# Experts of a decoder layer: five split weight halves of six, a written order for three engines, twelve raw pages

## The chip, the cores and the metric

The kernel runs on one core of one Trainium2 chip. The metric is device microseconds of one execution, median of three runs: 1540.11 us before the change (1538.99 to 1541.56).

## What is computed

One decoder layer over 1024 tokens of width 1024: an RMSNorm and a combined input projection, stick-breaking attention and an S5 state-space branch side by side, a gated merge and output projection, then a hierarchical mixture of experts and a final RMSNorm. The change is in the mixture of experts only:

```python
def hierarchical_moe(x, rg_w, rg_b, re_w, re_b, w1, w3, w2):
    # router: top-1 of 4 groups, then top-2 of the 8 experts in it; gate = p_group * softmax
    ...
    # each of the 32 experts: (silu(xe @ w1) * (xe @ w3)) @ w2, w1 and w3 1024 x 512, w2 512 x 1024
    ...
```

Tokens are routed in blocks of 128 rows: every expert takes the first 128 tokens that chose it; a rare overflow is handled in a branch at the end. All weights are float32.

## The kernel before

From 0 to about 862 us the kernel does everything ahead of the experts; the last part of that is a loop over eight token tiles that adds the output projection, writes the normed tokens to `hg_d` and computes the routing. Then `moe` runs 32 experts, one after the other, and ends with a sum over each token's two results, the final norm and the stores.

**An expert's weights** are six pages of 1 MB, halves of w1, w3 (k-blocks 0 to 3 and 4 to 7) and w2, loaded by SP's queue (L1052) into a ring of 14 raw pages: six named r, six m, two x. A load waits until its page is given back. A half is then either *split* or used *natively*. Split (`split`, L98 to L102): ScalarE copies it to a high part in fp32r (L101, CAST), VectorE subtracts that to make a low part (L102, TENSOR_TENSOR), and TensorE makes three fp32r products per k-block, high by high, high by low, low by high. Native: TensorE multiplies the float32 page itself (L1120, two records for each product). Before, the first halves of w1 and w3 and both halves of w2 are split, four of six; the second halves of w1 and w3 are native. Split parts live in three pairs of pages: two of name w, one of name ms.

**An expert's steps.** GpSimd gathers its 128 tokens by an indirect DMA (L1066). TensorE transposes them (L1088); ScalarE and VectorE make xh and xl (four k-blocks) and xf, the unsplit rest. `up` (L1112 to L1114 split, L1120 native) forms the two products a1 and a3; ScalarE's sigmoid (L1126) and two VectorE products (L1128) form the hidden tile in `mid`; TensorE transposes that (L1133), ScalarE and VectorE split it to hh and hl, and `down` (L1145 to L1147) multiplies by w2 into the two banks o0 and o1. ScalarE scales by the gate (L1152), GpSimd scatters the rows to `ye_d` (L1159). The last two experts' results stay on the chip.

**What sets the order.** `moe` is written with `down` one expert behind `up`; within that a scheduler, which simulates the engines, chose each engine's order when the kernel was built. Engines are in order, so what stands in front of a late instruction's followers holds them. For the first expert the lows of both first units are made on GpSimd (`HELD`, L102 with POOL), as routing occupies VectorE; and the first pages are loaded during the routing.

Of the kernel before, what the change touches and what calls it, by code (L numbers as in the profile page):

```python
# [22 lines left out]
D = 1024  # L23
# [10 lines left out]
NE = 32  # L34
# [960 lines left out]
def moe(tc, ctx, pool, i, ident, rt, ye_d, tab_d, h2_d, hg_d, split, con, out, rp, mp, wop, wop1, scale):  # L995
# [4 lines left out]
    XG, YB, NX, LAG = 3, 4, 2, 3  # L1000
    PS = (1, 3, 5)
    XL = 3, 3, 5, 5, 7, 7
    INIT = RING = 12 + NX
    HELD = 2
    LAST = 2
    with ExitStack() as c:
# [6 lines left out]
        xg, ss = row[:XG], p.tile([128, FF], F32, name="mid", bufs=1)  # L1013
# [9 lines left out]
        def add(key, ap, shape):  # L1023
            num[key] = len(src)
            src.append((ap, shape))

        for e in range(NE + 1):
            for u in range(2):
                for j, w in enumerate(w13):
                    if e < NE:  # L1030
                        add((e, u, j), w[e, :, u * 4:u * 4 + 4, :], [128, 4, FF])
            for u in range(2):
                if e:
                    add((e - 1, u, 2), w2[e - 1, :, u * 2:u * 2 + 2, :], [128, 2, D])
# [10 lines left out]
        def ring(n, shape, r=False):  # L1045
            k = n if n < INIT else (n - INIT) % RING
            return page(*((rp, "r", 6) if k < 6 else (mp, "m", MR) if k < 12 else (p, "x", NX)), shape, r)
# [28 lines left out]
        with tc.issue_after(rt["hold"]):  # L1076
            for n in range(HELD):
                unit(n)

        def xt(e):  # L1080

            x = xg[e % XG]
            xh, xl = (p.tile([128, 4, 128], F32R, name=n, bufs=1) for n in ("xh", "xl"))
            xf = p.tile([128, 4, 128], F32, name="xf", bufs=1)
            for q in range(2):
                tp = ps.tile([128, 4, 128], F32, name="tr", bufs=2)
                for k in range(4):
                    nc.tensor.transpose(tp[:, k], x[:, (q * 4 + k) * 128:(q * 4 + k) * 128 + 128], ident)  # L1088
                if q:
                    A.copy(xf, tp)  # L1090
                else:
                    parts[:] = split(xh, xl, tp)
            return xh, xl, xf

        gather(0)
        parts = []
        X = {0: xt(0)}
        read = rt["finish"](first[0], parts[1])
        with tc.issue_after(read):
            for n in range(12, INIT):  # L1100
                load(n)
        for n in range(1, XG):
            gather(n)
        for n in range(INIT, INIT + HELD):
            load(n)

        def up(e, xh, xl, xf):
            a = [ps.tile([128, 512], F32, name=n, bufs=2) for n in ("a1", "a3")]
            for w in range(2):
                h, l = unit(num[e, 0, w])  # L1110
                for k in range(4):
                    nc.tensor.matmul(a[w], lhsT=xh[:, k], rhs=h[:, k], start=(k == 0), stop=False)  # L1112
                    nc.tensor.matmul(a[w], lhsT=xh[:, k], rhs=l[:, k], start=False, stop=False)  # L1113
                    nc.tensor.matmul(a[w], lhsT=xl[:, k], rhs=h[:, k], start=False, stop=False)  # L1114
            yield
            for w in range(2):
                n = num[e, 1, w]
                load(n)
                for k in range(4):
                    nc.tensor.matmul(a[w], lhsT=xf[:, k], rhs=raws[n][:, k], start=False, stop=(k == 3))  # L1120
            yield

            s = ss.rearrange("p (k q) -> p k q", k=4)
            a = [x.rearrange("p (q k) -> p k q", k=4) for x in a]
            r = _f(tab[:, e, 3:4])
            A.activation(s, a[0], AF.Sigmoid, scale=r)  # L1126
            for n in range(2):
                V.scalar_tensor_tensor(s, a[n], r, s, op0=OP.mult, op1=OP.mult)  # L1128

        def ht():  # L1130
            tp = ps.tile([128, 4, 128], F32, name="tr", bufs=2)
            for k in range(4):
                nc.tensor.transpose(tp[:, k], ss[:, k * 128:k * 128 + 128], ident)  # L1133
            rooted[:] = split(hh, hl, tp)

        def down(e):
            o = [ps.tile([128, 512], F32, name=f"o{n}", bufs=1) for n in range(2)]
            for u in range(2):
                with tc.issue_after(rooted[0]) if e == NE - 1 and u else ExitStack():
                    h, l = unit(num[e, u, 2])  # L1140
                for n in range(2):
                    cs = slice(n * 512, n * 512 + 512)
                    for k in range(2):
                        kk = u * 2 + k
# [51 lines left out]
        for e in range(NE):  # L1196
            g = up(e, *X[e])
            next(g)
            if e:
                ht()  # L1200
# [201 lines left out]
```

## Time and profile before

| | us |
|---|---|
| median of 3 runs | 1540.11 |
| profiled execution, its own time | 1539.6 |
| its span in the profile | 1537.7 |
| TensorE busy | 1456.8 |
| VectorE busy | 963.0 |
| ScalarE busy | 722.3 |
| GpSimd busy | 518.9 |

The experts take from about 865 to 1493 us of the span, the part after them some 45 us. The mean granted TensorE clock is 0.974 of full speed. The DMA engines read 284.03 MB and write 44.11 MB; most of the reading is the experts' weights, in the last 16 of the profile's 40 slices. The span and the profiled execution's own time differ by 1.9 us; the profiled execution is 0.5 us under the median.

### The profile page before, as it was taken

The page shows a single profiled execution, that of the slowest core. Times are in us where ns is not written, and L with a number is a line of the kernel's source. Part 1 is how long each engine was busy: PE and PEld are TensorE (multiplying, and loading weights), DVE is VectorE, ACT ScalarE, POOL GpSimd, SP SyncE. Part 2 cuts the span into 40 slices and gives each one's busy share as a digit, 9 for nine tenths or more (in the row PEclk, how much of TensorE's full clock was granted, in tenths as well). Part 3 has the DMA queues.
Part 4 walks back from the last instruction along what each step waited for, and adds up shares of the span by engine and source line. Part 5 has one row for each costly group of instructions (what it writes and reads, how often), then busy time and mean ns, then how long its engine had stood idle before and what let it go on. Part 6 is the DMA issues. An engine that isn't in the chain of part 4 may idle for free. (4 is left out here: it accounts for less than half of the span.)

```text
span 1537.7 us, 19509 instructions
## 1 busy us (share of the span) xinstructions
PE 1456.8 (95%) x6900; PEld 1123.4 (73%) x6900; DVE 963.0 (63%) x1488; ACT 722.3 (47%) x1141; POOL 518.9 (34%) x542
## 2 busy tenths in 40 slices
PE   7989799999999989999998799999999999999986
PEld 6967688998888867778787566666666666666663
DVE  6757565465756568665578566666665566656547
ACT  6212122455656577432223255555555455555543
POOL 1199941144444465332255321111111111111034
PEclk8999899999999999999999799999999999999998
DMA  8242344211111015264763799999999989999754
GB/s 256 77 104 72 92 104 97 60 42 54 30 51 34 28 44 142 78 198 160 268 247 124 286 346 356 352 354 353 356 360 351 353 342 358 334 334 357 271 200 163
DMA packets 132197, 314.77 MB, mean 205 GB/s; under 512 B 24305, under 2 KB 82289, under 8 KB 107522
## 3 DMA queue, kind: packets, MB, share of 16 engines
q1 hardware_dynamic: 120898, 295.99, 55.0%
q0 software_dynamic: 9728, 16.83, 2.9%
q8 instruction: 55, 0.90, 0.2%
q10 hardware_dynamic: 1472, 0.69, 0.2%
q14 instruction: 44, 0.36, 0.1%
HBM read 284.03 MB, written 44.11 MB: 213 GB/s over the span
## 5 line engine op out<-in xcount | busy, mean ns | idle before, releaser
L134 PE MATMUL mm<-xh,wh 128*128 128x512 f32 (+4 forms) x608 | 224.1, 369 | 1.1 <-DVE kl L691 0.6
L135 PE MATMUL mm<-xl,wh 128*128 128x512 f32 (+4 forms) x608 | 222.6, 366 | 0.0
L136 PE MATMUL mm<-xh,wl 128*128 128x512 f32 (+4 forms) x608 | 221.3, 364 | 0.8 <-DVE wl L102 0.8
L1159 POOL DMA_INDIRECT ye_d<-w,tab x32 | 56.1, 1754 | 250.0 <-ACT w L1152 249.4
L134 PEld LDWEIGHTS mm<-xh,wh 128*128 128x128 f32 x608 | 115.4, 190 | 16.0 <-issue 1.1
L136 PEld LDWEIGHTS mm<-xh,wl 128*128 128x128 f32 x608 | 115.4, 190 | 14.9 <-DVE wl L102 1.5
L135 PEld LDWEIGHTS mm<-xl,wh 128*128 128x128 f32 x608 | 115.3, 190 | 13.9 <-DVE xl L225 0.4
L754 DVE TENSOR_TENSOR_SCAN pr<-pr 128x144 f32<-128x144 f32 (+3 forms) x64 | 92.6, 1448 | 46.8 <-POOL pr L751 46.1
L102 DVE TENSOR_TENSOR w<-m,w 128x2048 fp32r<-128x2048 f32 x38 | 88.9, 2342 | 40.8 <-ACT w L101 40.7
L102 DVE TENSOR_TENSOR w<-r,w 128x2048 fp32r<-128x2048 f32 x36 | 82.2, 2291 | 47.6 <-ACT w L101 47.2
L1066 POOL DMA_INDIRECT w<-hg_d,tab x31 | 34.8, 1122 | 222.0 <-PE tr L1088 217.1
L755 POOL TENSOR_TENSOR be<-be,pr 128x143 f32<-128x143 f32 (+3 forms) x64 | 89.4, 1400 | 38.4 <-DVE pr L754 36.0
L1120 PE MATMUL a<-r,xf 128*128 128x512 f32 x224 | 100.7, 592 | 0.0
L1120 PE MATMUL a<-m,xf 128*128 128x512 f32 x208 | 93.3, 592 | 0.0
L1128 DVE SCALAR_TENSOR_TENSOR mid<-a,tab,mid 128x512 f32<-128x512 f32 x64 | 47.9, 749 | 63.8 <-ACT mid L1126 52.0
L101 ACT CAST w<-r 128x2048 fp32r<-128x2048 f32 x38 | 72.1, 1903 | 27.5 <-PE a L1113 14.4
L101 ACT CAST w<-m 128x2048 fp32r<-128x2048 f32 x38 | 72.5, 1907 | 18.9 <-PE o L1146 10.3
L101 ACT CAST wh<-wr 128x1024 fp32r<-128x1024 f32 (+1 forms) x44 | 44.6, 1014 | 65.8 <-PE mm L135 57.3
L1120 PEld LDWEIGHTS a<-r,xf 128*128 128x128 f32 x224 | 41.8, 190 | 42.3 <-issue 40.4
L102 DVE TENSOR_TENSOR wl<-wr,wh 128x1024 fp32r<-128x1024 f32 (+1 forms) x44 | 57.1, 1297 | 23.6 <-ACT wh L101 23.5
L1146 PE MATMUL o<-w,w 128*128 128x512 f32 x172 | 68.6, 399 | 3.2 <-DVE w L102 3.2
L751 POOL TENSOR_SCALAR_AFFINE_SELECT pr<-pr 128x128 f32<-128x128 f32 x64 | 26.3, 411 | 132.9 <-ACT pr L748 113.1
(534 smaller groups left out, 3766.2 us busy)
## 6 DMA issues: line engine op xcount, KB each, us to landing
r<-in_w_dram SPq DMA_DIRECT2D x84, 1024.0 KB, 7.9
m<-in_w_dram SPq DMA_DIRECT2D x82, 1024.0 KB, 8.1
x<-in_w_dram SPq DMA_DIRECT2D x26, 1024.0 KB, 7.9
wr<-in_w_in_dram SPq DMA_DIRECT2D x32, 512.0 KB, 4.2
gate_d<-gt SPq DMA_DIRECT2D x32, 256.0 KB, 2.3
x<-in_x_dram SPq DMA_DIRECT2D x8, 512.0 KB, 4.6
y<-y_d SPq DMA_DIRECT2D x16, 256.0 KB, 3.2
wr<-in_w_out_dram SPq DMA_DIRECT2D x8, 512.0 KB, 4.3
```

Source lines behind the costliest of these rows:

```text
L101: a = (A if heng is None else heng).copy(h, src)
L102: return a.ins, (V if leng is None else leng).tensor_sub(l, src, _f(h)).ins
L134: nc.tensor.matmul(ps, lhsT=wh, rhs=xh, start=first, stop=False)
L135: nc.tensor.matmul(ps, lhsT=wh, rhs=xl, start=False, stop=False)
L136: nc.tensor.matmul(ps, lhsT=wl, rhs=xh, start=False, stop=last)
L754: V.tensor_tensor_scan(rv, rv, rv, 1.0, op0=OP.mult, op1=OP.bypass)
L755: P.tensor_mul(be[:, :W - 1], be[:, :W - 1], pr[:, 1:W])
L1066: q = P.indirect_dma_start(out=xg[e % XG], out_offset=None, in_=hg_d, in_offset=IO(ap=tab[:, e, 0:1] if e else rt["idx"], axis=0), bounds_ ...
L1120: nc.tensor.matmul(a[w], lhsT=xf[:, k], rhs=raws[n][:, k], start=False, stop=(k == 3))
L1128: V.scalar_tensor_tensor(s, a[n], r, s, op0=OP.mult, op1=OP.mult)
L1146: nc.tensor.matmul(o[n], lhsT=hh[:, kk], rhs=l[:, k, cs], start=False, stop=False)
L1159: put = P.indirect_dma_start(out=ye_d, out_offset=IO(ap=tab[:, e, 1:2], axis=0), in_=y, in_offset=None, bounds_check=2 * S - 1, oob_is_err ...
```

## The change

Within `moe`, and nowhere else:

- Weights: the second half of w1 is split too. Five of six halves are split; only w3's second half is native, 4 native products per expert where there were 8, and 60 split products where there were 48. xh and xl now hold all eight k-blocks.
- Pages: the two raw x pages become a fourth pair for split parts, and the pairs go round in the order x, w, w, ms. The raw ring has 12 pages, r and m.
- Order: a `manual_schedule` for TensorE, ScalarE and VectorE; their instructions are issued as the loop writes them. In iteration e: gate scaling and scatter of e−2; up(e,w1,0); up(e,w3,0); half of the transposes of e+1; the hidden tile of e−1 transposed and split; up(e,w1,1); the other transposes; down(e−1,0); the native half; down(e−1,1). Loads are issued in the order of use.
- The hidden tile is written in the row of the expert's result; the tile `mid` is gone.
- Start: units (0,w1,0) and (0,w3,0) have their lows on GpSimd, the first in pair x, the second in pair w; unit (0,w1,1) has its low on VectorE.
- End: as the engines' orders stand, both w2 halves of expert 31 are split ahead of the overflow branch, and the result of expert 30 is split behind it. Two of the eight tiles of `ye_d` rows go to x pages.

```diff
@@ constants
-    XG, YB, NX, LAG = 3, 4, 2, 3
+    XG, YB, LAG = 3, 4, 3
-    INIT = RING = 12 + NX
+    RING = 12
@@ units
-        def unit(n):
-            if n not in units:
-                load(n)
-                pl, nm, b = (mp, "ms", 2) if len(units) % 3 == 2 else (wop, "w", 4)
-                h, l = units[n] = [view(pl.tile([128, 4, FF], F32R, name=nm, bufs=b), src[n][1]) for _ in range(2)]
-                split(h, l, raws[n], leng=P if n < HELD else V)
-            return units[n]
+        PAIRS = (p, "x", 2), (wop, "w", 4), (wop, "w", 4), (mp, "ms", 2)
+        def unit(*key, other=False, later=False):
+            n = num[key]
+            load(n)
+            h, l = units[key] = [page(*PAIRS[len(units) % 4], src[n][1], True) for _ in range(2)]
+            A.copy(h, raws[n])
+            low = lambda: (P if other else V).tensor_sub(l, raws[n], _f(h))
+            return low if later else low()
@@ the order
+        with tc.manual_schedule(engines={mybir.EngineType.PE, mybir.EngineType.Activation, mybir.EngineType.DVE}):
+            unit(0, 0, 1)
+            for e in range(NE):
+                more = e + 1 < NE
+                acc[e] = [ps.tile([128, 512], F32, name=n, bufs=2) for n in ("a1", "a3")]
+                if e >= 2:
+                    result(e - 2)
+                up(e, 0, 0)
+                if e:
+                    unit(e - 1, 2, 0)
+                up(e, 1, 0)
+                if e:
+                    low = unit(e - 1, 2, 1, later=True)
+                if more:
+                    tp = xt(e + 1, 0)
+                if e:
+                    th = turn(ys(e - 1), 0)
+                if more:
+                    xparts(tp, 0)
+                if e:
+                    split(hh, hl, th)
+                    low()
+                if more:
+                    unit(e + 1, 0, 0)
+                up(e, 0, 1)
+                if more:
+                    tp = xt(e + 1, 1)
+                    xparts(tp, 1)
+                    unit(e + 1, 1, 0)
...
+                if e:
+                    down(e - 1, 0)
+                if more:
+                    unit(e + 1, 0, 1)
+                native(e)
+                mid = middle(e)
+                next(mid)
+                if more:
+                    A.copy(xf, tp)
+                drain(mid)
+                if e:
+                    down(e - 1, 1)
...
         overflow(at)
-        ht()
-        parted()
+        th = turn(ys(NE - 1), 0)
+        rooted[:] = split(hh, hl, th)
+        result(NE - 2)
+        for u in range(2):
+            unit(NE - 1, 2, u)
```

How the instructions stand. In the names, a is a product of `up`, o one of `down`, tr a bank of transposes, w_86.. a row tile (tokens, result or hidden parts), r, m, x, w, ms the pages.

TensorE in the middle of a steady expert, around one native half; before:

```order
L1114 MATMUL a_9242<-w,xl 128x512
L1133 MATMUL tr<-ident,mid 128x128 x3
L1112 MATMUL a_9243<-w,xh 128x512
L1133 MATMUL tr<-ident,mid 128x128
L1120 MATMUL a_9242<-r,xf 128x512 x4
L1088 MATMUL tr<-ident,w_8634 128x128
L1113 MATMUL a_9243<-w,xh 128x512
```

and after:

```order
L1095 MATMUL tr<-ident,w_8635 128x128 x4
L1136 MATMUL o_9537<-ms,w_8641 128x512
...
L1138 MATMUL o_9538<-ms,w_8641 128x512
L1116 MATMUL a_9447<-r,xf 128x512 x4
L1136 MATMUL o_9537<-x,w_8641 128x512
L1137 MATMUL o_9537<-x,w_8641 128x512
```

Before, native products and transposes stand between split products of the same bank; after, the one native half stands whole between the two halves of `down` (L1136 to L1138), in every expert alike.

ScalarE over one expert; before:

```order
L101 CAST ms<-m 128x2048
L101 CAST xh<-tr 128x512
L1090 COPY xf<-tr 128x512
L101 CAST w<-m 128x2048
L1152 ACTIVATE w_8637<-o_9077,tab 128x512
L101 CAST w<-x 128x2048
L1152 ACTIVATE w_8637<-o_9078,tab 128x512
L101 CAST ms<-x 128x2048
L101 CAST w_8641<-tr 128x512
L1126 ACTIVATE mid<-a_9120,tab 128x512
```

and after:

```order
L1145 ACTIVATE w_8639<-o_9404,tab 128x512
L1145 ACTIVATE w_8639<-o_9405,tab 128x512
L1067 CAST ms<-r 128x2048
L1067 CAST x<-r 128x2048
L101 CAST xh<-tr 128x512
L101 CAST w_8641<-tr 128x512
L1067 CAST w<-r 128x2048
L101 CAST xh<-tr 128x512
L1067 CAST w<-r 128x2048
L1067 CAST ms<-m 128x2048
L1123 ACTIVATE w_8637<-a_9446,tab 128x512
L1236 COPY xf<-tr 128x512
```

The gate scalings (L1145) move to the head of the iteration after, five weight casts stand where four did, and the hidden tile's cast (w_8641) now stands behind two of them and ahead of three.

GpSimd at the end of routing; hg is the normed tile, tab_d the table of places, w_8634 to w_8636 the token rows of the first gathers. Before:

```order
L102 TENSOR_TENSOR w<-r,w 128x2048
L875 TENSOR_TENSOR hg<-h_8382,g_7242 128x8x64
L102 TENSOR_TENSOR w<-r,w 128x2048
L875 TENSOR_TENSOR hg<-h_8382,g_7242 128x8x32
L1016 MEMSET w_8634 128x1024
...
L1066 DMA w_8634<-hg_d,idx 128x1024
L987 DMA tab_d<-pay,rows 32768x4 x2
...
L1066 DMA w_8635<-hg_d,tab 128x1024
```

and after:

```order
L1068 TENSOR_TENSOR w<-r,w 128x2048
L875 TENSOR_TENSOR hg<-h_8382,g_7242 128x8x64
L1017 MEMSET w_8634 128x1024
L875 TENSOR_TENSOR hg<-h_8382,g_7242 128x8x32
...
L1074 DMA w_8634<-hg_d,idx 128x1024
L987 DMA tab_d<-pay,rows 32768x4 x2
L1068 TENSOR_TENSOR x<-r,x 128x2048
L1074 DMA w_8635<-hg_d,tab 128x1024
```

One low stays where both stood; the other, x, stands behind the last puts (L987) and ahead of the second gather.

## Rows read from the trace of the kernel before

**Rows 1.** Page, part 1: busy us, share of the span, instructions.

```profile
PE 1456.8 (95%) x6900; PEld 1123.4 (73%) x6900; DVE 963.0 (63%) x1488; ACT 722.3 (47%) x1141; POOL 518.9 (34%) x542
```

**Rows 2.** Windows: length, busy PE PEld DVE ACT POOL, PEclk, DMA share, GB/s.

```profile
880.00:1280.00 400.00, 400.00 (x1590) 275.99 (x1589) 242.18 (x166) 226.63 (x206) 68.47 (x45) 1.00 0.94 353
1280.00:1480.00 200.00, 194.96 (x759) 131.86 (x757) 118.89 (x82) 109.87 (x101) 22.57 (x19) 1.00 0.82 305
```

**Rows 3.** Waits, 900 to 1470, TensorE's longest: us in total, times, longest one.

```profile
PE o L1146 <- DVE w L102: 2.4, 4, 1.2
```

**Rows 4.** Timeline, GpSimd: start, us, what, idle before.

```profile
958.66 2.33 POOL L1159 DMA_INDIRECT ye_d<-w,tab  x1 [6.73 <-ACT w L1152]
...
977.78 2.33 POOL L1159 DMA_INDIRECT ye_d<-w,tab  x1 [6.73 <-ACT w L1152]
```

**Rows 5.** Timeline, TensorE: last product of experts 0 and 30.

```profile
898.31 0.39 PE L1147 MATMUL o<-ms,w 128*128 128x512 f32 x1
...
1478.50 0.40 PE L1147 MATMUL o<-ms,w 128*128 128x512 f32 x1
```

**Rows 6.** Timeline, TensorE: split and native products of one expert.

```profile
1108.92 0.39 PE L1112 MATMUL a<-ms,xh 128*128 128x512 f32 x1
...
1111.65 0.49 PE L1133 MATMUL tr<-ident,mid 128*128 128x128 f32 x3
...
1112.32 3.60 PE L1120 MATMUL a<-m,xf 128*128 128x512 f32 x8
1115.76 0.27 PE L1088 MATMUL tr<-ident,w 128*128 128x128 f32 x1
```

**Rows 7.** Lines, 850 to 1537, by form: busy, mean ns, idle before.

```profile
L102 DVE TENSOR_TENSOR w<-m,w 128x2048 fp32r<-128x2048 f32 x38 | 88.9, 2342 | 40.8 <-ACT w L101 40.7
L101 ACT CAST w<-m 128x2048 fp32r<-128x2048 f32 x38 | 72.5, 1907 | 18.9 <-PE o L1146 10.3 <-PE a L1113 8.5
L1128 DVE SCALAR_TENSOR_TENSOR mid<-a,tab,mid 128x512 f32<-128x512 f32 x64 | 47.9, 749 | 63.8 <-ACT mid L1126 52.0 <-PE a L1120 11.9
L1152 ACT ACTIVATE w<-o,tab 128x512 f32<-128x512 f32 x64 | 43.8, 685 | 23.6 <-PE o L1147 23.6
L102 DVE TENSOR_TENSOR xl<-tr,xh 128x512 fp32r<-128x512 f32 x32 | 21.9, 685 | 13.9 <-ACT xh L101 12.4 <-PE tr L1088 1.5
```

**Rows 8.** Loads, L1052 from 880 to 1470; windows, the fastest five us.

```profile
DMA to landing us min/median/max: 4.9/8.0/11.6
...
985.00:990.00 5.00, 5.00 (x21) 3.07 (x20) 3.55 (x3) 2.46 (x3) 0.85 (x1) 1.00 1.02 419
```

**Rows 9.** Timeline, end of routing and expert 0; last, gathers of 860 to 882.

```profile
831.68 4.59 POOL L102 TENSOR_TENSOR w<-r,w 128x2048 fp32r<-128x2048 f32 x1
835.25 7.53 DVE L960 TENSOR_SCALAR dl<-lg,mg 128x4 f32<-128x4 f32 x1
862.46 0.97 POOL L987 DMA_INDIRECT tab_d<-pay,rows  x1 [0.30 <-issue]
863.45 0.19 DVE L909 TENSOR_SCALAR ov<-ov 128x32 f32<-128x32 f32 x1
864.17 1.07 PE L1088 MATMUL tr<-ident,w 128*128 128x128 f32 x8 [1.22 <-DVE nov L911]
865.52 0.50 PE L1112 MATMUL a<-w,xh 128*128 128x512 f32 x1 [0.28 <-ACT xh L101]
867.53 1.03 POOL L1066 DMA_INDIRECT w<-hg_d,tab  x1 [3.74 <-DMA tab<-tab_d]
879.27 0.50 PE L1112 MATMUL a<-ms,xh 128*128 128x512 f32 x1 [0.24 <-ACT xh L101]
...
DMA to landing us min/median/max: 4.3/6.4/8.7
```

**Rows 10.** Timeline, the end of the experts.

```profile
1486.29 4.25 DVE L102 TENSOR_TENSOR w<-m,w 128x2048 fp32r<-128x2048 f32 x1 [1.10 <-ACT w L101]
...
1490.60 0.50 PE L1146 MATMUL o<-w,w 128*128 128x512 f32 x1 [0.80 <-DVE w L102]
```

More of the change, by code (lines that the diff above doesn't have):

```diff
@@ L1076, in moe @@
         with tc.issue_after(rt["hold"]):
[L1077 to L1104, printed above, removed]
-            load(n)
[L1107 to L1124, printed above, removed]
@@ new lines, in moe, with turn, xt @@
+            unit(0, 0, 0, other=True)
+            unit(0, 1, 0, other=True)
+        xh, xl = (p.tile([128, KD, 128], F32R, name=n, bufs=1) for n in ("xh", "xl"))
+        xf = p.tile([128, 4, 128], F32, name="xf", bufs=1)
+        def turn(x, c0):
+            tp = ps.tile([128, 4, 128], F32, name="tr", bufs=2)
+            for k in range(4):
+                nc.tensor.transpose(tp[:, k], x[:, c0 + k * 128:c0 + k * 128 + 128], ident)
+            return tp
+        def xt(e, q):
+            return turn(xg[e % XG], q * 512)
@@ L1128, in up, with down @@
                 V.scalar_tensor_tensor(s, a[n], r, s, op0=OP.mult, op1=OP.mult)
[L1130 to L1144, printed above, removed]
[L1145 to L1147 removed]
+        def down(e, u):
+            if u == 0:
+                o[:] = [ps.tile([128, 512], F32, name=f"o{n}", bufs=1) for n in range(2)]
+            h, l = units[e, 2, u]
+            for n in range(2):
+                cs = slice(n * 512, n * 512 + 512)
+                for k in range(2):
+                    kk = u * 2 + k
+                    nc.tensor.matmul(o[n], lhsT=hh[:, kk], rhs=h[:, k, cs], start=(kk == 0), stop=False)
+                    nc.tensor.matmul(o[n], lhsT=hh[:, kk], rhs=l[:, k, cs], start=False, stop=False)
+                    q = nc.tensor.matmul(o[n], lhsT=hl[:, kk], rhs=h[:, k, cs], start=False, stop=(kk == 3))
@@ L1163, in scatter @@
             puts.append(put.ins)
-        def ahead(e):
-            for n in range(num[e, 0, 0], len(src)):
-                load(n)
         def places():
@@ L1192, in overflow @@
             more_blocks(tc, c, pool, p, [row[2], row[5], row[6], at[:, 0]], ps, i, ident, rt, nov, hg_d, ye_d, tab_d)
-        puts, done, rooted = [], [], []
-        last = {}
[L1196 to L1199, printed above, removed]
-                ht()
-            if e == NE - 1:
-                ahead(e)
-                hot, at = places()
-                res = tiles(len(src) + 2, h2_d, 0)
-            drain(g)
-            if e + XG < NE:
-                gather(e + XG)
-            if e + 1 < NE:
-                X[e + 1] = xt(e + 1)
-            if e:
-                parted = down(e - 1)
-            if e == 1:
-                zero = ys(3)
-                P.memset(zero, 0.0)
-                with tc.issue_after(first[-1]):
-                    for n in range(NE - LAST, NE):
-                        scatter(n, zero)
@@ L1224, in moe @@
             n = len(src) + 6 + t
-            bs.append([ring(n + k, [128, 2, D]) for k in range(2)])
+            bs.append([ring(n + k, [128, 2, D]) if t < 6 else page(p, "x", 2, [128, 2, D]) for k in range(2)])
             for k in range(2):
@@ L1229, in moe @@
                     nc.sync.dma_start(bs[-1][b][:, k], ye_d[r:r + 128, :])
-        parted = down(NE - 1)
-        parted()
+        for u in range(2):
+            down(NE - 1, u)
+        result(NE - 1)
         gf = at[:, 1]
```

86 lines of the change are left out of this document (64 added, 22 removed).

## The prediction

> **What bounds the kernel now.** First the page's busy shares [rows 1]: TensorE is the busiest engine, with VectorE, ScalarE and GpSimd far below it. A share over the whole span hides stages, so next the table by windows of the stage that the change touches, the experts [rows 2]: from 880 to 1280 us TensorE is busy 400 of 400 us at granted clock 1.00; from 1280 to 1480 us it loses 5.04 us. The waits of this stage [rows 3] say the same: TensorE's longest wait is 2.4 us in all, for a low half of w2. So an expert takes as long as TensorE's own instructions, and the change is to be costed in them. Loads are issued when a page is given back, so a shorter period makes them come faster by itself; whether the queues can follow is costed below.
>
> The period is read from the scatter, once per expert [rows 4]: 977.78 − 958.66 = **19.12 us**. The last product of expert 0 starts at 898.31 and that of expert 30 at 1478.50 [rows 5], 580.2 us for 30 experts. Thirty periods of 19.12 are 573.6, less 1.0 for the last of them, which has no x to transpose (eight transposes, 1.07 [rows 9]), make 572.6: the late experts cost 7.6 us more than steady ones, of which 5.0 show as TensorE idle [rows 2].
>
> **The matmuls.** Both forms stand side by side in one expert [rows 6]. Twelve split products (four k-blocks, three each) start at 1108.92 and the next instruction at 1111.65: 2.73 us, 0.2275 each. Four native products (eight records) run from 1112.32 to 1115.76: 3.44 us. The change makes w1's second half split: 3.44 − 2.73 = 0.71 us less per expert, so the period becomes **18.41 us** as long as nothing else takes over. Over 30 experts that is −21.3 us.
>
> **What must keep up.** Durations are those of [rows 7], per expert after the change.
> - VectorE: five weight lows at 2.34 or less, two x lows and one hidden low at 0.69, two SwiGLU products at 0.75: at most 11.7 + 2.1 + 1.5 = 15.3 of 18.4 us.
> - ScalarE: five weight casts at 1.91, and at the 0.69 of a gate scaling, which is of the same size, two of those, the sigmoid, two x casts, the hidden cast and the xf copy: 9.55 + 7 × 0.69 = 14.4 of 18.4 us.
>
> Neither becomes the bound by sum; an in-order engine may still be late at one point, so I followed one iteration of the written order, from the start of up(e,0,0) as zero. ScalarE: result(e−2) until 1.4, the cast of the first w2 half until 3.3, of the second until 5.2 (its pair is given back by up(e,0,0) at 2.7). TensorE turns x and the hidden tile by 6.2; ScalarE casts them until 7.2, VectorE makes xl and then hl by 7.9. TensorE meanwhile has up(e,0,1) and four transposes and reaches down(e−1,0) at 9.3. **hl has 1.4 us to spare**, the tightest place. The second w2 low ends at 10.2 and is wanted at 15.5; the last low for the next expert ends at 17.8 and is wanted some 6 us into the next iteration; the SwiGLU products then end 0.9 us into the next iteration and are turned at 5.8 of it. So I cost the extra split at nothing: TensorE's own work covers it, and if hl's cover went, each us beyond 1.4 would be a us per expert. The gate scalings come an iteration later, but nothing waits for a scatter before the output, and the o banks that they give back at 1.4 are wanted at 9.3.
>
> **The late experts.** The order of before was made by a scheduler, and its late low halves (ScalarE and VectorE working on something else first) are the 7.6 us. The written order is the same for every expert, so I take them as gone: −7.6. Bounds: 0 and −7.6. Both parts together: −21.3 − 7.6 = **−28.9**.
>
> **Loads and pages.** Twelve raw pages for fourteen. A load lands 8.0 us after issue at the median [rows 8]; six loads per expert and twelve pages give a page a life of two periods, 36.8 us; less the 8.0 of the load that leaves nearly 29 us for landed data to wait and be split. The data rate must rise from 353 GB/s [rows 2] by 19.12/18.41 to 367. The row that shows a higher rate is the 5 us at 419 GB/s with DMA share 1.02 [rows 8]; no row shows how long such a rate would hold. I take a cost of 0; the bounds are 0 and rival 2.
>
> **The head.** Before, both first units had their lows on GpSimd, 4.59 us each; while they ran, VectorE's L960 took 7.53 us from 835.25, to the end of the second one [rows 9]. After, the page pairs begin with x, and only the w low stands there; a VectorE low of 2.3 us for (0,0,1) comes in its stead. That brings the end of routing forward by 4.5 − 2.3 = 2.2 to 4.5 us; I take 3.5, since the memsets are spread too. But the x low, of the very first unit that TensorE multiplies, now stands on GpSimd behind the last two puts: in old times it would run from 863.4 (862.46 + 0.97) to 868.0, where the first product used to start at 865.52, and its second needs that low. It also stands ahead of gather 1, which issued at 867.53 [rows 9]. Counting with everything 3.5 earlier: the low ends at 864.5, up(0,0,0) and up(0,1,0) at 869.7, gather 1 is issued at 864.5 and lands 6.4 us later, the median of the first gathers [rows 9], at 870.9; four transposes, 12 split products, four transposes and the four native products (0.5 + 2.7 + 0.5 + 3.4) then end at 878.0, and expert 1 starts there, against 879.27 before: −1.2. It would be less if VectorE's L909, at 863.45 before and so where the x low would start, is held to the low's end as L960 was: TensorE's first turn of x was waiting for the count that L909 leads to, the first product would come at 866.4 and, after 5.5 + 0.5 + 2.7 + 0.5 + 3.4, expert 1 at 878.9: −0.4. The 7.53 us of L960 show that VectorE can be held so; the Trainium skill, SBUF — State Buffer, section SBUF: two separate sides, has the reason: the port pair that the two engines share goes whole to whoever starts first, for the whole instruction. By that rule the smaller gain holds, without it the larger. Between the two I take −0.8, and with the 0.7 that iteration 1 itself saves the end of expert 0's down comes **1.5** earlier. Bounds: −4.5 (the full routing gain kept, and no stall) and +3 (no gain at all in routing, x low and gather 1 fully in the way).
>
> **The tail.** Before, the split of expert 30's result stands ahead of the overflow branch, and the second half of expert 31's w2 is split behind it beside GpSimd's adds, where the low takes 4.25 us in place of 2.29 and TensorE waits 0.80 [rows 10]. After, both w2 halves are split ahead of the branch and the result's parts behind it; of those only one low of half that size can be stretched. I take −1.5. Bounds: −4 (the slowed low and its wait both gone and the branch reached sooner) and +1 (the result's low is stretched and wanted at once).
>
> **The sum.** −28.9 − 1.5 − 1.5 = −31.9 on the profiled execution's 1539.6 us (span 1537.7): 1507.7. The median of the runs is 0.5 above the profiled time: **1508**. A difference below 0.2%, about 3 us, is what a measurement of this kernel can't tell from no change.
>
> **The rivals.**
> 1. Late experts stay late. For it: why those lows were late is not in the rows; if a transfer was, the written order does not cure it. Against it: the pages have nearly 29 us. 1508 + 7.6 = **1515.6**; with the upper bounds of head and tail 1522. Chance 0.15.
> 2. The loads become the bound. If the queues can give no more than the 353 GB/s that rows 2 show, an expert takes 19.1 us to load; 30 × 0.71 = 21 us of lag gather by the end, of which the 29 us above, less the 4.3 of a cast and its low, swallow all: 1508. If the rate fell to 340, as nothing in rows 2 shows for long stretches but nothing excludes, a period would be 19.12 × 353/340 = 19.85: 43 us of lag less 25 make 18, **1526**. It decides from a sustained rate of some 350. Chance 0.07.
> 3. **Slower**: the written order makes TensorE wait at down(e−1,0) for hl in every expert. TensorE follows the order, so nothing of the next expert can fill the gap, as the old order let up products do. It decides from 1.4 + 31.9/30 = 2.5 us of lateness in each expert; a cast of a weight half and its low that get in ahead of the hidden tile's parts, because the ones before them ran late (1.91 + 2.34 = 4.25), would give 1508 + 30 × (4.25 − 1.4) = **1593**. For it: ScalarE and VectorE have only 3 to 4 us of slack per expert and run in order, and my count has no time for the steps between engines. Against it: the second low stands behind hl in the order, and what TensorE, ScalarE and VectorE handed on in [rows 9] came within 0.3 us. Chance 0.05.
> 4. The split products cost no less than the native: then only head, tail and late experts gain, 1508 + 21.3 = 1529. Against it stands the pair in [rows 6], from one expert. Chance 0.02.
>
> The forecast itself has 0.71, and its own range, by the bounds of head and tail, (−4.5 + 1.5 and −4 + 1.5; +3 + 1.5 and +1 + 1.5) is 1502.5 to 1515. To hold 8 in 10 the range takes in rival 1 with a part of them, and about a us more at the lower end for lows that turn out cheaper: **1501 to 1520**. Faster by over 0.2%: the forecast and rivals 1, 2 and 4 make 0.95. Of rival 3's 0.05, 0.01 is for a mild form that ends within 0.2%: same 0.01, slower 0.04.
>
> **What would show it.** Scatters 18.4 us apart from 900 to 1450; TensorE busy without gaps there and in the former late stretch; VectorE at 15 us per expert; the last product of expert 30 near 1448; expert 1's first product near 878. Wrong if TensorE shows a wait per expert at the first product of down, if scatters drift apart late (rivals 1, 2: then the releaser is a DMA or a low), or if the split products of w1's second half are longer than 0.23 us apart.

## The result, and the profile after

The changed kernel takes **1512.95 us** (median of four runs, 1510.91 to 1514.95) against 1539.55 for the kernel before beside it: a ratio of 0.9825, interval 0.9808 to 0.9842. The forecast was 1508, the range 1501 to 1520. It is faster, as forecast, by 26.6 us where the sum had 31.9.

The profiled execution (1512.5 us, span 1510.7) is 27.0 shorter in span than before's. Where that comes from is read at two instructions, the last product of expert 0 and that of expert 30:

| part of the span, us | before | after | difference | forecast |
|---|---|---|---|---|
| up to expert 0's last product | 898.31 | 898.07 | −0.24 | −1.5 |
| from there to expert 30's last product | 580.19 | 552.96 | −27.2 | −28.9 |
| from there to the end | 59.2 | 59.67 | +0.5 | −1.5 |

So the experts give all of it. Part 1 of the page of after, for [rows 1]:

```profile
PE 1429.9 (95%) x7028; PEld 1146.3 (76%) x7028; DVE 1043.2 (69%) x1552; ACT 799.6 (53%) x1205; POOL 502.0 (33%) x542
```

TensorE has 128 instructions more and is busy 26.9 us less; VectorE has 80 us more. That 26.9 comes so near to the whole gain is chance: between the two instructions of the table TensorE is busy 576.25 us before and 552.96 after, 23.3 less, and the other 3.9 us of the experts' gain are waits that are gone (580.19 − 576.25); the rest of the 26.9 lies at the ends. The windows of after, for [rows 2] (same columns):

```profile
880.00:1280.00 400.00, 400.00 (x1741) 304.14 (x1740) 315.08 (x220) 293.17 (x263) 52.24 (x46) 1.00 0.97 373
1280.00:1440.00 160.00, 160.00 (x690) 120.82 (x690) 123.87 (x86) 115.59 (x104) 20.24 (x17) 1.00 0.92 350
```

TensorE has no gap in either stretch; before, it lost 5 us in the later one, 3.9 of them ahead of expert 30's last product and 1.1 behind it. The data rate is up from 353 to 373 GB/s, and a weight load takes longer to land (loads of L1058, 880 to 1470), for [rows 8]:

```profile
DMA to landing us min/median/max: 6.6/9.2/13.4
```

The timeline of GpSimd in after, first and last scatter of a regular run, for [rows 4]:

```profile
936.38 0.99 POOL L1152 DMA_INDIRECT ye_d<-w,tab  x1 [8.46 <-ACT w L1145]
...
1434.91 0.98 POOL L1152 DMA_INDIRECT ye_d<-w,tab  x1 [16.48 <-ACT w L1145]
```

These are 27 periods: 498.53 / 27 = **18.46 us**, and 30 of them less 1.07 make 552.9, what the experts took (552.96). The stretched late experts are gone. TensorE in a steady expert of after, for [rows 6], and the two ends of [rows 5]:

```profile
898.07 0.39 PE L1138 MATMUL o<-ms,w 128*128 128x512 f32 x1
...
1107.63 0.48 PE L1108 MATMUL a<-w,xh 128*128 128x512 f32 x1
1107.95 0.39 PE L1109 MATMUL a<-w,xh 128*128 128x512 f32 x1
...
1110.47 0.60 PE L1095 MATMUL tr<-ident,w 128*128 128x128 f32 x4
...
1451.03 0.39 PE L1138 MATMUL o<-w,w 128*128 128x512 f32 x1
```

The twelve products of the newly split half run from 1107.63 to 1110.47: 2.84 us, not the 2.73 of [rows 6]. They stand between two banks of transposes, and the first product after a bank takes 0.32 until the next one starts, where the others take 0.23 (2.84 − 0.32 over eleven).

The head of after, timelines of GpSimd, VectorE and TensorE, for [rows 9]:

```profile
860.22 4.51 POOL L1068 TENSOR_TENSOR x<-r,x 128x2048 fp32r<-128x2048 f32 x1
860.63 4.15 DVE L908 TENSOR_SCALAR ov<-ov 128x32 f32<-128x32 f32 x1
862.26 0.50 PE L1108 MATMUL a<-x,xh 128*128 128x512 f32 x1 [0.28 <-ACT xh L101]
864.79 0.49 PE L1109 MATMUL a<-x,xh 128*128 128x512 f32 x1 [2.03 <-POOL x L1068]
864.90 1.04 POOL L1074 DMA_INDIRECT w<-hg_d,tab  x1 [0.16 <-issue]
866.10 0.80 PE L1110 MATMUL a<-x,xl 128*128 128x512 f32 x1 [0.81 <-DVE xl L102]
...
869.25 0.40 PE L1108 MATMUL a<-x,xh 128*128 128x512 f32 x1
...
879.39 0.79 PE L1108 MATMUL a<-ms,xh 128*128 128x512 f32 x1
```

The first product comes 3.3 us earlier than before (862.26 for 865.52), and expert 1 starts 0.1 later (879.39 for 879.27). The second product waits for GpSimd's x low, the third for xl, which stands behind the count on VectorE: L908 there, an instruction on 128x32, takes 4.15 us and ends with that low. After the two waits seven products, from 866.10 on, take 3.15 us, 0.43 from start to start once the first is past: the granted clock is 0.50 from 866.00 to 869.25, the lower of TensorE's two levels, and 1.00 after it.

The tail of before, behind [rows 10], timelines of TensorE, GpSimd and VectorE:

```profile
1492.78 0.39 PE L1147 MATMUL o<-w,w 128*128 128x512 f32 x1
...
1498.42 9.35 POOL L1253 TENSOR_TENSOR m<-m,r 128x1024 f32<-128x1024 f32 x4
1500.39 0.69 DVE L1263 TENSOR_TENSOR r<-r,a 128x512 f32<-128x512 f32 x1 [4.17 <-PE a L1262]
...
1532.73 1.29 DVE L130 SCALAR_TENSOR_TENSOR m<-m,rr 128x1024 f32<-128x1024 f32 x1
```

and of after:

```profile
1453.54 0.66 PE L1095 MATMUL tr<-ident,w 128*128 128x128 f32 x4 [2.12 <-DVEq L1327]
...
1461.81 0.39 PE L1138 MATMUL o<-ms,w 128*128 128x512 f32 x1
...
1469.00 1.48 DVE L1299 TENSOR_TENSOR m<-m,a 128x512 f32<-128x512 f32 x2 [3.74 <-PE a L1298]
...
1481.66 2.39 POOL L1289 TENSOR_TENSOR m<-m,r 128x1024 f32<-128x1024 f32 x1
...
1484.10 3.33 DVE L130 SCALAR_TENSOR_TENSOR m<-m,rr,r 128x1024 f32<-128x1024 f32 x1
...
1493.42 2.34 POOL L1289 TENSOR_TENSOR x<-x,r 128x1024 f32<-128x1024 f32 x1
...
1505.39 1.28 DVE L130 SCALAR_TENSOR_TENSOR x<-x,rr,r 128x1024 f32<-128x1024 f32 x1
```

Expert 31's last product starts 10.8 us after expert 30's (1461.81 − 1451.03), where it was 14.3 before (1492.78 − 1478.50), and VectorE's final chain (adding the last experts' rows, norm, scale) starts 18.0 after expert 30's instead of 21.9 (1469.00 − 1451.03 for 1500.39 − 1478.50): 3.9 us gained. But the chain takes 37.7 us, 1469.00 to 1506.7, where it took 33.6. Three of GpSimd's eight adds of the result rows (L1289, before L1253) now start well inside it, the last at 1493.42; before, all were done at 1507.8, early in a chain from 1500.39 to 1534.0. VectorE's instructions beside GpSimd's are stretched there: L130 takes 3.33 instead of 1.28. What L130 and the two kinds of 128x1 SCALAR_TENSOR_TENSOR take in the chain beyond their shortest (1.28, 0.22 and 0.16) adds up to 11.0 us in after and 7.1 before: 3.9 of the chain's 4.0.

### The profile page after: what moved, and what is told of

It reads as the page before. It is cut to its first block, busy times and chain, and to the rows that moved or that the text cites. A ratio compares the mean times of both kernels' runs of the same rounds, so it can differ in the third digit from the quotient of the medians.

```text
span 1510.7 us, 19933 instructions
## 1 busy us (share of the span) xinstructions
PE 1429.9 (95%) x7028; PEld 1146.3 (76%) x7028; DVE 1043.2 (69%) x1552; ACT 799.6 (53%) x1205; POOL 502.0 (33%) x542
## 5 line engine op out<-in xcount | busy, mean ns | idle before, releaser
L135 PEld LDWEIGHTS mm<-xl,wh 128*128 128x128 f32 x608 | 115.7, 190 | 14.4 <-DVE xl L225 1.0
L1152 POOL DMA_INDIRECT ye_d<-w,tab x32 | 33.3, 1040 | 271.1 <-ACT w L1145 270.5
L1074 POOL DMA_INDIRECT w<-hg_d,tab x31 | 40.5, 1307 | 207.2 <-PE tr L1095 205.9
L1068 DVE TENSOR_TENSOR w<-r,w 128x2048 fp32r<-128x2048 f32 x39 | 92.7, 2378 | 16.3 <-ACT w L1067 16.3
L102 DVE TENSOR_TENSOR xl<-tr,xh 128x512 fp32r<-128x512 f32 x64 | 43.9, 688 | 58.2 <-ACT xh L101 58.2
L101 ACT CAST xh<-tr 128x512 fp32r<-128x512 f32 x64 | 37.5, 587 | 78.0 <-PE tr L1095 74.2
L1067 ACT CAST w<-r 128x2048 fp32r<-128x2048 f32 x40 | 76.3, 1908 | 3.8 <-PE mm L871 3.1
L1108 PE MATMUL a<-w,xh 128*128 128x512 f32 x196 | 77.8, 397 | 0.0
L1067 ACT CAST w<-m 128x2048 fp32r<-128x2048 f32 x40 | 76.5, 1911 | 0.8
L1110 PE MATMUL a<-w,xl 128*128 128x512 f32 x196 | 76.6, 391 | 0.0
L1109 PE MATMUL a<-w,xh 128*128 128x512 f32 x196 | 76.4, 390 | 0.0
L102 DVE TENSOR_TENSOR wl<-wr,wh 128x1024 fp32r<-128x1024 f32 (+1 forms) x44 | 57.2, 1299 | 24.6 <-ACT wh L101 24.5
L1145 ACT ACTIVATE w<-o,tab 128x512 f32<-128x512 f32 x64 | 44.2, 690 | 53.1 <-PE o L1138 53.1
```

What stands on the lines that cost most here:

```text
L101: a = (A if heng is None else heng).copy(h, src)
L102: return a.ins, (V if leng is None else leng).tensor_sub(l, src, _f(h)).ins
L135: nc.tensor.matmul(ps, lhsT=wh, rhs=xl, start=False, stop=False)
L1067: A.copy(h, raws[n])
L1068: low = lambda: (P if other else V).tensor_sub(l, raws[n], _f(h))
L1108: nc.tensor.matmul(acc[e][w], lhsT=xh[:, kk], rhs=h[:, k], start=(kk == 0), stop=False)
```

## The experiments

The theory: TensorE's own instructions set the experts' time, the split half is worth about 0.67 us per expert, and the written order removes the stretched late experts. The rivals: the loads bind; the order alone or the split alone does it; the hidden tile's low (hl) is near the edge. After that the two ends, where the forecast was off.

**1. The order without the split half.** w1's second half is native again, in the written order; the new pages, pairs and ends stay.

```diff
-                up(e, 0, 1)
+                native(e, 0)
```

(and the units of that half are not made.)

> The written order with w1's second half native again (8 native products per expert, 4 splits, as before the change). Theory A (the gain is TensorE's own work plus the even order): the period goes from 18.46 back to 19.12 us, 0.66 more in each of 32 experts, without longer late experts: 1513 + 21 = 1534 us (1531 to 1537). Theory B (the gain is the written order, the split half only moves work): at most 1518 us.

Measured: 1531.22, ratio to before 0.994 (0.9923 to 0.9956). GpSimd's timeline, two scatters 21 experts apart:

```profile
1052.92 1.00 POOL L1152 DMA_INDIRECT ye_d<-w,tab  x1 [6.93 <-ACT w L1145]
...
1454.82 0.98 POOL L1152 DMA_INDIRECT ye_d<-w,tab  x1 [14.25 <-ACT w L1145]
```

The period is 401.9 / 21 = 19.14, the 19.12 of before, and it holds to the end. So the order, with the pages that come with it, is worth 8.6 us (1539.79 − 1531.22), the late experts; the split half is worth 18.3 between medians, 19.14 − 18.46 = 0.67 per expert.

**2. The split half without the order.** Everything as after, but the three engines' orders are chosen by the scheduler.

```diff
-        with tc.manual_schedule(engines={mybir.EngineType.PE, mybir.EngineType.Activation, mybir.EngineType.DVE}):
+        with ExitStack():
```

> The changed kernel without the written order: the scheduler chooses, with five splits, four pairs and twelve pages. Theory A: TensorE's work is the same, so 18.4 to 18.5 us per expert as long as lows come in time, and some late lows as in the kernel before: 1513 to 1523 us. Theory B (ScalarE and VectorE have so little slack that only this order holds the pace): over 1535 us, with TensorE waiting for lows in every expert.

Measured: 1558.76, ratio 1.0128 (1.0111 to 1.0145): **slower than before**. The windows, and TensorE's longest wait from 900 to 1430:

```profile
880.00:1280.00 400.00, 386.06 (x1636) 287.97 (x1635) 297.12 (x207) 268.85 (x248) 73.20 (x44) 0.99 0.92 345
1280.00:1440.00 160.00, 151.84 (x630) 111.07 (x629) 112.82 (x79) 102.36 (x95) 24.13 (x17) 0.98 0.90 332
```

```profile
PE a L1108 <- ACT w L1067: 5.7, 4, 1.7
```

and a wait of ScalarE, from 900 to 1440:

```profile
ACT w L1067 <- PE o L1137: 25.6, 16, 5.0
```

TensorE loses 22 us in 560, and its granted clock is 0.99 and 0.98 there; the longest waits are for casts, shorter ones for lows. From 905 to 1100 us it has no gap, and nine experts take 18.6 us each on average: the split half pays there too. The late casts begin behind that, and from the last product of expert 0 to that of expert 30 it is 590.3 us (905.44 to 1495.76), 10.1 more than before; another 7.1 of the 19 us lie ahead of expert 0's last product. What the casts waited for is TensorE's own `down` products, which give a pair of pages back; no load is among their releasers, so the shorter ring is not what holds them. The split half removes TensorE work only; it adds a cast and a low per expert, and without the written order they come late. The two parts of the change are worth −18.3 and −8.6 with the order, and +19 for the split and the pages without it. A scheduled order with the new pages and four splits was not run, so how much of the 19 is the fifth split's is not shown.

**3. hl late in every expert.** The hidden tile's split is put behind the second w2 low and the next expert's first one, which brings rival 3 about.

```diff
                 if e:
-                    split(hh, hl, th)
                     low()
                 if more:
                     unit(e + 1, 0, 0)
+                if e:
+                    split(hh, hl, th)
```

> The hidden tile's split is put behind the second w2 low and the first low of the next expert; no work is added. If the count of slack is right (hl ends 1.85 us before the product that reads it, and would now end 2.7 us after it), TensorE waits some 2.7 us at down in each expert: period 21.2 us, 1513 + 30 x 2.7 = 1594 us. If there is hidden slack elsewhere: no change, 1513 us.

Measured: 1608.47 (a single run; 1594 was expected), 95.5 above after, 3.2 per expert. TensorE's longest wait from 900 to 1470, and timelines of TensorE and VectorE:

```profile
PE o L1138 <- DVE w L102: 61.5, 26, 2.4
```

```profile
1089.44 0.63 PE L1138 MATMUL o<-ms,w 128*128 128x512 f32 x1
...
1091.14 4.45 PE L1116 MATMUL a<-r,xf 128*128 128x512 f32 x8
...
1105.52 4.48 DVE L1068 TENSOR_TENSOR w<-m,w 128x2048 fp32r<-128x2048 f32 x2
1107.90 0.40 PE L1137 MATMUL o<-x,w 128*128 128x512 f32 x1
1109.92 0.68 DVE L102 TENSOR_TENSOR w<-tr,w 128x512 fp32r<-128x512 f32 x1
1110.66 0.50 PE L1138 MATMUL o<-x,w 128*128 128x512 f32 x1 [2.36 <-DVE w L102]
```

From 1107.90 to 1110.66 are 2.76 us in place of 0.23, so a late hl costs 2.53 per expert. In after hl ends at 1109.44 (start 1108.76, 0.68) and its product starts at 1111.38, a slack of 1.9; two lows, 4.48, less 1.9 are 2.6. The rest is the clock: in every third expert the products after the wait stand 0.43 apart from 1089.44 and the eight native records take 4.45 (3.60 otherwise), at a granted clock of 0.66 from 1089.44 to 1094.44; the scatters are then 22.7 apart, otherwise 21.1, a mean of 0.5. So rival 3's mechanism is real. The forecast's 2.85 per expert (4.25 − 1.4) were 2.53 for the wait and some 0.5 for the clock, which it did not have.

**4. A smaller ring.** The weight loads go round in eight of the twelve pages, so a page's life falls from 36.9 us to 8/6 of a period, 24.6.

```diff
-            return page(*((rp, "r", 6) if n % RING < 6 else (mp, "m", MR)), shape, r)
+            return page(*((rp, "r", 6) if n % (8 if n < len(src) else RING) < 6 else (mp, "m", MR)), shape, r)
```

> Weight loads go round 8 pages in place of 12 (six r, two m in eight), so each is issued some 12 us later. If loads have spare time (life of a page 8/6 of 18.46 = 24.6 us, less 9.2 landing, less 4.2 for cast and low: 11 us left): no change, 1513 us within 3. If the loads are at their limit at 0.97 of the queues: spacing of 19 us and over, 1530 us or more.

Measured: 1510.27, ratio 0.9812 (0.9795 to 0.9828), no difference from after that the intervals show; in the profile VectorE's final chain is 1.8 us shorter (35.9). First window:

```profile
880.00:1280.00 400.00, 400.00 (x1738) 303.48 (x1737) 314.58 (x221) 292.98 (x262) 52.67 (x46) 1.00 0.96 373
```

TensorE stays at 400 of 400 and the rate at 373 GB/s. The loads do not bind, and after has at least the 12 us to spare by which a page's life was cut (36.9 − 24.6).

**5 and 6. The head, twice missed.** In h1 the page pairs go round as w, w, ms, x: no GpSimd low stands ahead of gather 1, and two lows are VectorE's. In h2, besides, the first expert's up(0,0,1) goes ahead of the transposes that wait for gather 1.

```diff
-        PAIRS = (p, "x", 2), (wop, "w", 4), (wop, "w", 4), (mp, "ms", 2)
+        PAIRS = (wop, "w", 4), (wop, "w", 4), (mp, "ms", 2), (p, "x", 2)
...
-            unit(0, 1, 0, other=True)
+            unit(0, 1, 0)
+            unit(0, 0, 1)
...
+                if not e:
+                    up(e, 0, 1)
```

> Only the start changes: pairs go round w, w, ms, x, so no unit of expert 0 uses pair x; the low of (0,w1,0) stays early on GpSimd, those of (0,w3,0) and (0,w1,1) go to VectorE behind routing. No low stands between the last puts and gather 1. Theory A (the x low on GpSimd cost the start its gain: 2.0 us of waiting for it, 0.8 for xl behind the held L908, some 1.6 us of products at half clock after the waits, and a VectorE low that took 5.9 us in routing): first product near 858 in place of 862.3, expert 1 starts near 873 in place of 879.4, waiting for gather 1; 1507 us (1504 to 1510). Rival (the start is set by the chain of puts, table and gather 1, whatever the lows do): within 2 us of 1513.

> As the run with the pairs turned, and expert 0's w1 second half is multiplied ahead of the transposes that need gather 1. Theory A: that covers what is left of the wait for gather 1, expert 1 starts near 871: 1505 us (1501 to 1508). Rival (expert 1's splits are then the late ones): no better than the run with the pairs turned alone.

Measured: 1516.27 (0.9856, 0.984 to 0.9873) and 1516.85 (0.9839, 0.9815 to 0.9863), no gain. Expert 1 starts at 879.08 and 880.01, where 873 and 871 were expected and after has 879.39. h1's profiled execution was the fastest of its four (1512.19), so its rows tell why nothing was gained, not where the 3.3 us of its median above after come from. Timelines of h1, then of after:

```profile
853.70 2.28 DVE L1068 TENSOR_TENSOR w<-r,w 128x2048 fp32r<-128x2048 f32 x1
854.58 2.32 POOL L1074 DMA_INDIRECT w<-hg_d,idx  x1 [5.21 <-DVE idx L982]
863.16 1.94 PE L1096 MATMUL tr<-ident,w 128*128 128x128 f32 x8 [4.24 <-DMA w<-hg_d,idx]
868.00 1.04 POOL L1074 DMA_INDIRECT w<-hg_d,tab  x1 [7.65 <-DMA tab<-tab_d]
```

```profile
856.54 1.04 POOL L1074 DMA_INDIRECT w<-hg_d,idx  x1 [5.02 <-DVE eps L1281]
...
860.91 1.07 PE L1095 MATMUL tr<-ident,w 128*128 128x128 f32 x8 [0.55 <-DMA w<-hg_d,idx]
```

Gather 0's issue takes 2.32 beside a VectorE low, where it took 1.04 in after. By the Trainium skill, SBUF — State Buffer, section SBUF: two separate sides, GpSimd cannot write the descriptors of its DMAs while VectorE runs an operation in a two-port mode, such as an fp32 copy. The row agrees in kind, for an operation that the sentence doesn't name, a subtraction with two inputs: the issue ends 0.92 after the low (856.90 for 855.98), about what an undisturbed one takes. Then gather 0 lands 6.3 us after its issue ends (856.90 to 863.16), in after 3.3 (857.58 to 860.91), and the table that gather 1 needs is there at 868.00; in after it was there by 864.90, when GpSimd came free. The reading of it: VectorE's early lows give raw pages back, and the weight loads that were waiting for them go ahead of gather and table; the DMA engines move 298 GB/s from 860 to 865, and 18 in after. The next run takes both away.

**7. The head with that mended.** As h2, but the weight loads are issued behind the table's load, and VectorE's lows, those of expert 1's first two units among them, stand behind the count (L911) and the token's xl. The edit is shown against h2.

```diff
+        with tc.issue_after(rt["novi"]):
             unit(0, 1, 0)
-            unit(0, 0, 1)
...
-        rt["finish"](first[0], x[1][1])
+        with tc.issue_after(x[1][1]):
+            unit(0, 0, 1)
+        with tc.issue_after(rt["finish"](first[0], x[1][1])):
+            for n in range(RING, RING + 2):
+                load(n)
```

> The start again, with what the run with the pairs turned seemed to collide with taken away: loads of new weight pages are queued behind the load of the table, and VectorE's lows stand behind the count that L907 to L911 make, so not beside gather 0 and the puts on GpSimd. Theory A (there, pages given back early let weight loads in ahead of gather 0 and the table, which then landed some 4 us later, and VectorE's lows made gather 0's issue take 2.3 us in place of 1.0): gather 0 lands 4.5 us after its issue as in the changed kernel, first product near 860, expert 1 starts near 874 in place of 879.4; 1507 us (1504 to 1511). Rival (gather 0 and the table are late for another reason): expert 1 no earlier than 877, 1511 us or more.

Measured: **1509.14**, ratio 0.9792 (0.9775 to 0.981), 3.8 under after. Timelines of GpSimd and TensorE, and a window:

```profile
854.00 1.04 POOL L1074 DMA_INDIRECT w<-hg_d,idx  x1 [5.22 <-DVE eps L1290]
...
861.33 1.04 POOL L1074 DMA_INDIRECT w<-hg_d,tab  x1 [3.69 <-DMA tab<-tab_d]
...
874.22 0.80 PE L1109 MATMUL a<-x,xh 128*128 128x512 f32 x1
```

```profile
1450.00:1455.00 5.00, 5.00 (x17) 3.92 (x15) 1.79 (x3) 1.33 (x2) 1.50 (x1) 0.66 0.99 338
```

Gather 0's issue is 1.04 again, gather 1 goes out at 861.33 in place of h1's 868.00, and expert 1 starts at 874.22, 5.2 before after's 879.39. Of that, 1.0 already stands ahead of all that the edit touches (GpSimd's normed tile at 835.53, in after at 836.54). Not all of the 5.2 reaches the end (3.8 between the medians, 2.7 between the profiled spans): behind the overflow branch TensorE's granted clock is 0.66 for 5 us, where after has 1.00, and expert 31's last product comes 12.35 behind expert 30's (1458.18 − 1445.83) in place of 10.8; the final chain starts another 0.9 later behind it. Which of the two mended things, lows or loads, does more was not tried apart.

**8 and 9. The tail, missed, then mended.** In t1 the overflow branch stands in the middle of expert 31, and the first loads of the result rows start behind it, so that GpSimd's adds are done before VectorE's final chain. In t2 a copy of the branch's counter is the first instruction behind the branch on ScalarE and VectorE, and expert 31's work is written behind that; the last low of expert 30's w2 stands ahead of hl there.

```diff
+                if not more:
+                    part.close()
+                    overflow(at)
+                    for b in range(2):
+                        fetch(0, b, rows_of(0, b))
+                    part.enter_context(order())
```

```diff
-                    overflow(at)
+                    it = overflow(at)
...
+                    for eng in (A.copy, V.tensor_copy):
+                        eng(p.tile([128, 1], F32, name="past", bufs=2), it)
```

> Only the end changes: the overflow branch stands in the middle of expert 31, after its w1 products, and the loads of the 8 MB of result rows begin behind it as pages come free, in place of behind expert 30's down (1453.7). Theory A (the tail's gain was given back because these loads, 20 us at 415 GB/s, and GpSimd's adds behind them begin no earlier in relation to the branch, and three adds fall beside VectorE's final chain): branch near 1442, TensorE loses 1 us there, adds done before the final chain, 1505 us (1499 to 1509). Rival (the final chain of VectorE and ScalarE sets the end by itself): 1510 to 1512, with only TensorE's wait at the branch saved.

> The branch in the middle of expert 31 again; a small copy that reads the branch's own counter now stands first behind it on ScalarE and VectorE, so that expert 31's w2 splits and SwiGLU can't be put ahead of it, which made TensorE wait 6.4 us there. Theory A: the branch is passed near 1444, TensorE loses about 1 us, the result rows load from 1444.5, GpSimd's adds end before VectorE's final chain, which takes 29 us in place of 37.7: 1505 us (1502 to 1509). Rival (the final chain is as long whatever comes ahead): 1511 to 1513.

Measured: t1 1512.55 (0.982, 0.9803 to 0.9836), no gain over after; t2 **1506.55** (0.9776, 0.976 to 0.9793), 6.4 under it. Timelines of VectorE and TensorE in t1:

```profile
1442.67 4.48 DVE L1068 TENSOR_TENSOR w<-m,w 128x2048 fp32r<-128x2048 f32 x2
...
1450.53 0.80 PE L1136 MATMUL o<-x,w 128*128 128x512 f32 x1 [6.43 <-DVEq L1347]
```

and of TensorE, GpSimd and VectorE in t2:

```profile
1444.93 0.50 PE L1136 MATMUL o<-x,w 128*128 128x512 f32 x1 [2.15 <-issue]
...
1465.59 5.69 POOL L1314 TENSOR_TENSOR m<-m,r 128x1024 f32<-128x1024 f32 x2
...
1470.26 0.69 DVE L1324 TENSOR_TENSOR m<-m,a 128x512 f32<-128x512 f32 x1 [3.55 <-PE a L1323]
...
1497.90 1.28 DVE L130 SCALAR_TENSOR_TENSOR x<-x,rr,r 128x1024 f32<-128x1024 f32 x1
```

In t1 expert 31's lows, which nothing tied to the branch, were moved ahead of it, and TensorE's next product waits for VectorE's side of the branch: it stood 6.4 us and came back at the lower level (granted clock 0.50 from 1450 to 1455). In t2 it stands 2.15, what the branch costs in after too (2.12), but the granted clock is 0.66 from 1445 to 1450, where after kept 1.00. The adds are done at 1471.3, and the final chain takes 28.9 us (1470.26 to 1499.2) against 37.7. t1, for all its loss at the branch, has the adds done before the chain too (1476.2 for 1476.8), and its chain takes the same 28.9 (1476.81 to 1505.73). In both, the stretches that came to 11.0 us in after come to 3.2: the adds beside the chain were what stretched it.

**10 and 11. Both ends together.** b1 is h2 with t1; b2 is h3 with t2. In both, the last result rows go to w pages in place of x pages.

> The start of the second run and the end of the third together. If both theories hold and are independent, the gains add: 1513 - 8 - 8 = 1497 us (1490 to 1505).

> Both of these together; if the two gains add, 1513 - 6 - 8 = 1499 us (1494 to 1506).

Measured: b1 1513.01 (0.9826, 0.981 to 0.9842), no gain, like its parts; b2 **1499.39** (0.9731, 0.9715 to 0.9748), 13.6 under after and 41 under the before beside it (1540.26), the fastest of all. The parts would give 10.2, and those of b1 1516.5: both kernels come 3.4 below the sum of their parts. Both have the w pages for the last rows; and in h3's profile 2.5 us of the head's gain were lost again in after's tail, which b2 doesn't have. No run tests either.

## Why the forecast came out, and where it was off

- **What bounds.** TensorE's own time, as forecast: 400 of 400 us busy before and after, and no rival to it in experiment 4.
- **The matmuls: direction right, size a little off.** 30 × 0.71 = −21.3 was taken; the period fell by 0.66, which is −19.7. The 2.73 us of [rows 6] belong to products that follow other split products; in the new place the half starts behind a bank of transposes and takes 2.84. But the old order paid for such places too, three times an expert, the new one twice. Priced from start to start in the expert of [rows 6] and in the one from 1101.40 to 1119.85 of after, the twelve products more cost 2.67 (48 took 11.20, 60 take 13.87), the four native ones less save 3.44 (with what the product behind them loses), and the transposes cost 0.08 more (1.15 for 1.07): 0.69 in all. So both terms were nearly right and the transposes were left out; the hundredths down to 0.66 are at the limit of what these rows tell.
- **What must keep up: right.** VectorE took 315.08 / 400 of 18.46, 14.5 us per expert (at most 15.3), ScalarE 13.5 (14.4). hl's slack was 1.9, forecast 1.4.
- **The late experts: right**, and shown by experiment 1: the period 19.14 holds to the end, and 8.6 us go (7.6 taken). It has the new pages as well as the order; experiment 2 has the pages without the order, and its experts are late. The reading "5.0 show as TensorE idle" takes in 1.1 behind expert 30's last product; 3.9 belong to the 7.6.
- **Loads and pages: right.** 373 GB/s held for 400 us; landing rose from 8.0 to 9.2 us at the median, 13.4 at most, which the page's life covers.
- **The head: too hopeful.** The step "four transposes, 12 split products, …" had expert 1 at 878.0 to 878.9; it came at 879.39. The routing gain was there (3.3 of 3.5), and the x low ended where the sum put it (864.73 for 864.5). The sum has both first units done at 869.7, ahead of gather 1's landing at 870.9, which sets the rest; they were done at 872.71. Of these 3.0 us, 1.1 are the third product's wait for xl and 1.6 the clock, which the sum did not have: seven products in 3.15 us in place of 1.59. VectorE was held to the low's end, as in the sum's smaller case, but what that case prices didn't happen: there the first turn of x waits for the count and the first product comes at 866.4; in after the first turn waits for gather 0 only, and the held L908 delays xl. That the port pair goes whole to whoever starts first, the rule that the prediction took from the Trainium skill (SBUF — State Buffer, section SBUF: two separate sides), agrees with L908's 4.15 us, which end with the low. Iteration 1 then gave 0.36 of the 0.7 taken (18.68 us from expert 1's first product to expert 0's last, for 19.04), as its first product now stands behind native ones and takes 0.64 to the next start in place of 0.34.
- **The tail: wrong in sign.** The step priced the split lows and the branch only, and stopped at TensorE's wait. That part came near its best bound, −3.9 for −4. The end is set by VectorE's final chain, and there the adds that moved beside it took 4.0 back; behind the chain the stores took 0.4 more. The step left out what comes after expert 31's last product; experiments 8 and 9 show the adds to be the cause. Head and tail together were forecast at −3.0 and came at +0.2, which the bounds given for them had room for.
- **The rivals.** 1 (late experts stay) and 2 (loads bind) fell with experiments 1 and 4, 4 (split no cheaper) with the 18.3 us of experiment 1. 3 did not occur, but its mechanism costs what was said and more (experiment 3). The rival that was not on the list is experiment 2's: five splits in a scheduled order, 19 us slower than before. The forecast treated split and order as two sums; over the whole run the order is the condition of the other.

## What to carry to other kernels

Where one engine is busy all the time, count its own instructions in the place where they will stand, and then find the tightest hand-off from the in-order engines that feed it: its slack tells whether the saving arrives, and a written order may be the condition for it. At the two ends of a pipeline follow the chain to the last instruction: work that is moved earlier in one place lands beside something else. And an experiment that moves work across a branch needs something that ties the work to its side of it.

## What the runs showed of the hardware that was not expected

- A wait of some 2 us on TensorE can cost more than itself, but doesn't each time: in experiment 3, with a wait of 2.36 in every expert, every third expert took 1.6 us more with a stretch at the lower clock level (22.7 against 21.1); in after's head, 2.03 and 0.81 of waiting were followed by seven products at that level. Behind the overflow branch, waits of 2.15 were followed by a granted clock of 0.66 over 5 us in h3 and t2, the 2.12 of after by 1.00.
- VectorE's instructions stretch beside GpSimd's, down to one on 128x32 that took 4.15 us (0.20 in before, with no GpSimd low beside it), and GpSimd's DMA issue stretches beside VectorE's lows, from 1.04 to 2.32.
- 373 GB/s were sustained over 400 us beside a fully busy TensorE; in after's tail, while the result rows came in, it was 415 from 1465 to 1470.
